# Three-branch decoder layer: idle transposes ahead of the first key products, key transposes tied behind twelve gate products, and a weight load that borrows the keys' buffer

## The chip, the core and the metric

The kernel runs on one core of one Trainium2 chip. The metric is the device time of one execution in microseconds; before the change it is 1395.42 us, the median of three runs.

## The reference, cut to what matters

One decoder layer over 1024 tokens of width 1024, in float32, with three token mixers side by side:

```python
h = rms_norm(x, g_norm)
proj = h @ w_in                       # split into the pieces named below
o_a = dsa_attention(q_a, k_a, v_a, q_i, k_i, w_i)   # 8 heads; a ReLU indexer picks the top 256 keys
o_b = causal_attention(q_b, k_b, v_b)               # 8 heads, low-rank q and kv, rotary part of 32
o_m = attention of q_m over 256 memory tokens       # 4 heads; k_m, v_m = rms_norm(mem) @ w_mem_kv
ys = [o_a * silu(z_a), o_b * silu(z_b), o_m * silu(z_m)]
branch[n] = ys[n] @ w_branch[n]
merged = sum over n of sigmoid(gate_logits[n]) * branch[n]
out = x + merged @ w_out
```

## The kernel before, in words

**Products.** Each float32 matrix is split into a high part and the rest (`wsplit`, line 242: ScalarE casts the high half, L243, VectorE or GpSimd subtracts for the low half, L246). A product is then three matmuls, high by high, high by low, low by high (`mm3`, L280 to L282). `wload` (line 248) takes a raw buffer from a pool, issues the loads on SyncE's queue (L260), takes two buffers for the halves and splits.

**Stages in order.** (1) The start: an identity matrix, 16 transposes of it into nowhere (L145), the memory tokens transposed (`norm_T`, L348, name `m`), the memory keys' products (`mkps`), the first four row blocks of x normalised and transposed (`x0tp`), the memory values' products (`mvps`), the rest of x, the memory queries. (2) The memory attention. (3) The latent projections of branch B and its queries. (4) Attention B (line 1047). (5) The indexer's projection and scores, and the first part of the top-k. (6) Branches M and B to the end, with the query/key/value projections of branch A (`qkv(p)`, line 1403, one for each of four pairs of heads) in between, and the top-k's steps spread over them on VectorE and ScalarE (`run_topk`). (7) Attention A (line 1596). (8) Branch A, and the output projection.

**Gate products.** The merge gates' logits have no order of their own and fill gaps of TensorE: `Filler.run(n)` (line 386) issues up to n products of 128 x 128 by 128 x 512, eight to a half job, and after eight ScalarE takes a tanh (L380) and SyncE stores it. A job is 16 products, and attention B has eight jobs, 128 products.

**`attention`** (line 545) serves B and A. Before its loop it generates the first pair's keys and values, calls `k_prep(0, 0)` (the first head's keys: eight transposes, L996 in B, L1525 in A, with copies) and `q_prep`, and runs gate products at four places in numbers given by a tuple, `PREB` or `PREA`:

```python
        for _ in load_ahead():
            fill.run(pre[0])
        ahead = load_ahead()
        fill.run(pre[1])
        k_prep(0, 0)
        fill.run(pre[2])
        q = q_prep(*units[0])
        fill.run(pre[3])
```

The loop has 33 steps; in B each runs three more gate products, and `fill.finish()` issues what is left. In B the keys of a pair come from the products `kv` (line 954); GpSimd multiplies them by their factors (L979, L981, tile `xk`).

**The last projection, `qkv(3)`.** Its weights come in four pieces (a3w0 to a3w3, three loads each) through two raw buffers, which the weights of the gate paths z use too, so a piece can be loaded only when the one two places before it has been split. Right behind it the keys of attention A's first pair are loaded (`load_k(0)`, line 1464, tile `akd`, tag `kd`, one buffer of 8 KB in each partition) and its queries (`load_q`, tile `aqs`), both tied behind the last of the weights' loads.

**What sets the order.** The program traces instructions in the order of the code; a scheduler then writes each engine's queue, by its own estimate of when an instruction is ready, so a gate product that stands later in the code can be issued before a transpose. `tc.issue_after(ins)` ties what a block issues on the engine of `ins` behind `ins`, in order only. Each engine works off its queue in order. A pool's tile with a tag of n buffers waits for the readers of the tile n places before it.

Of the kernel before, what the change touches and what calls it, by code (L numbers as in the profile page):

```python
# [11 lines left out]
F32 = mybir.dt.float32  # L12
# [11 lines left out]
P = 128  # L24
NT = S // P
# [9 lines left out]
WSM = [1]  # L35
WSB = [1]
WSI = [1]
PREB = (0, 0, 0, 16)
PREA = (0, 0, 4, 4)
NFQ = 2  # L40
PFQ = 4
NZG = 3
NWU = 16
WSF = [1]
WSO = [1]
ZB5 = 4
# [54 lines left out]
def hybrid_kernel(  # L101
# [5 lines left out]
    nc = tc.nc  # L107
    x, mem, out = x[0], mem[0], out[0]
    w_in, w_uq, w_ukv, w_mem_kv, w_branch, w_out = (
        w_in[0], w_uq[0], w_ukv[0], w_mem_kv[0], w_branch[0], w_out[0])  # L110
# [13 lines left out]
    def ps_t(nm, dt=F32):  # L124
        return pp.tile([P, 512], dt, tag="tp", name=nm, bufs=NTP)

    def ps_f(nm):
        return pp.tile([P, 512], F32, tag="fl", name=nm, bufs=1)
# [11 lines left out]
    ident = cp.tile([P, P], F32, name="ident")  # L140
    make_identity(nc, ident)
    identr = cp.tile([P, P], FR, name="identr")
    nc.vector.tensor_copy(identr, ident)
    for i in range(NWU):
        nc.tensor.transpose(ps_t(f"wu{i}")[:, 0:P], ident, ident)  # L145
    ones = cp.tile([P, 1], BF, name="ones")
    nc.vector.memset(ones, 1.0)
    mhalf = cp.tile([P, 128], F32, name="mhalf")
# [96 lines left out]
        eng = nc.vector if ws[wcount[0] % len(ws)] else nc.gpsimd  # L245
        eng.tensor_tensor(lo, raw, f(hi), op=ALU.subtract)  # L246

    def wload(pool, nm, srcs, a, n, kind=None):


        def tile(dt, tag, bufs, nm, width):
            if width is None:
                return pool.tile([P, a, n], dt, tag=tag, name=nm, bufs=bufs)
            t = pool.tile([P, width], dt, tag=tag, name=nm, bufs=bufs)
            return t[:, 0:a * n].rearrange("p (a n) -> p a n", a=a)
        width = pool_raw[2] if len(pool_raw) > 2 else None
        raw = tile(F32, "raw", pool_raw[0], nm + "r", width)
        o = 0
        for ap, w in srcs:
            last_load[0] = nc.sync.dma_start(raw[:, :, o:o + w], ap)  # L260
            o += w
        tag, bufs, width = kind or ("wp", pool_raw[1], width)
        hi = tile(FR, tag, bufs, nm + "h", width)
        lo = tile(FR, tag, bufs, nm + "l", width)
        if nm == "mkw0":
            for i in range(2):
                wsplit(hi[:, i], lo[:, i], raw[:, i])
        else:
            wsplit(hi, lo, raw)
        return hi, lo  # L270

    pool_raw = list(PRM)
# [3 lines left out]
    def wview(w, k0, a, c0, n):  # L276
        return w[k0 * P:(k0 + a) * P, c0:c0 + n].rearrange("(a p) c -> p a c", p=P)

    def mm3(ps, ah, al, bh, bl, start, stop):
        nc.tensor.matmul(ps, ah, bh, start=start, stop=False)  # L280
        nc.tensor.matmul(ps, ah, bl, start=False, stop=False)  # L281
        nc.tensor.matmul(ps, al, bh, start=False, stop=stop)  # L282

    def proj_w(nm, pool, w, cols, nk, per=None, held={}):

# [51 lines left out]
    def norm_T(xp, xs, tbs, gcol, dst, nm, scale=True):  # L337

        for tb, xt in zip(tbs, xs) if scale else ():
            r = sm.tile([P, 1], F32, tag="xr", name=f"{nm}r{tb}")  # L340
            row_factor(xp, xt, f"{nm}{tb}", r)
            eng = nc.gpsimd if tb in NXP else nc.vector
            eng.tensor_scalar(out=xt, in0=xt, scalar1=r, scalar2=None, op0=ALU.mult)
        n = len(tbs) * P
        for k in range(NK):
            tp = ps_t(f"{nm}tp{k}")
            for i, xt in enumerate(xs):
                nc.tensor.transpose(tp[:, i * P:(i + 1) * P], xt[:, k * P:(k + 1) * P], ident)  # L348
            hi, lo = dst(k)
            hi_ins.append(nc.scalar.activation(hi, tp[:, 0:n], AF.Copy, scale=gcol[:, k:k + 1]))  # L350
            nc.vector.scalar_tensor_tensor(out=lo, in0=tp[:, 0:n], scalar=gcol[:, k:k + 1], in1=f(hi),
                                           op0=ALU.mult, op1=ALU.subtract)
# [192 lines left out]
    def attention(gen, k_prep, q_prep, scores, pv, fill, per, pre, GEN, ldj):  # L545

        units = [(p, hh, G) for p in range(4) for hh in range(2) for G in GORD]
        pairs = iter(range(4))

        def load_ahead():  # L550
            p = next(pairs, None)
            if p is None:
                return iter(())
            g = gen(p)
            next(g)
            return g

        for _ in load_ahead():
            fill.run(pre[0])
        ahead = load_ahead()  # L560
        fill.run(pre[1])
        k_prep(0, 0)
        fill.run(pre[2])
        q = q_prep(*units[0])
        fill.run(pre[3])
        N = len(units)

        def fl(k):

            nonlocal ahead  # L570
            want = go + (GEN[j] - go) * sum(GF[:k + 1]) / sum(GF)
            while done[0] < want and next(g, 0) != 0:
                done[0] += 0.5
            if k == 4 and j == ldj:
                for _ in g:
                    pass
                ahead = load_ahead()
            fill.run(per[k])
        Sc, V = None, None
        for i in range(N + 1):  # L580
            j = i % 8
            if j == 0:
                g, done = ahead, [0]
            go = done[0]
            Sn = scores(*units[i], q) if i < N else None
            V = pv(*units[i - 1], Sc) if 1 <= i <= N else None
            if Sn:
                Sn.mm(0)
            if V:
                V.pt(0)  # L590
            fl(0)
            if Sn:
                Sn.exp(0)
                Sn.mm(1)
            if V and V.nk > 1:
                V.pt(1)
            fl(1)
            if Sn:
                Sn.exp(1)
                Sn.norm()  # L600
            if V:
                for kp in range(2, V.nk):
                    V.pt(kp)
                    fl(kp)
                    V.mmv(kp - 2)
                if V.nk > 1:
                    V.mmv(V.nk - 2)
            fl(4)
            if i < N:
                if j == KP1:  # L610
                    k_prep(units[i][0], 1)
                if j == 7 and i + 1 < N:
                    k_prep(units[i][0] + 1, 0)
                if i + 1 < N:
                    q = q_prep(*units[i + 1])
            fill.run(per[5])
            if V:
                V.mmv(V.nk - 1)
            if V:
                V.evac()  # L620
            Sc = Sn
        fill.finish()
# [8 lines left out]
    with ExitStack() as ph:  # L631
        wpool = ph.enter_context(tc.tile_pool(name="w1", bufs=3, reuse_waits="tile"))
# [30 lines left out]
        with ExitStack() as ph2:  # L663
# [52 lines left out]
            for i in range(2):  # L716
                raw = hT_first[i]
# [10 lines left out]
            for kp in range(NK // 2):  # L728
                raw = wpool.tile([P, 2, 544], F32, tag="raw", name=f"mvw{kp}", bufs=PRM[0])
# [16 lines left out]
            for h in range(4):  # L746
                tp = ps_t(f"kmt{h}")
# [6 lines left out]
        with ExitStack() as ph2:  # L754
# [19 lines left out]
            for j in range(2):  # L774
                for h in range(4):
                    tbs = range(4 * j, 4 * j + 4)
                    nm = f"m{h}_{j}"
                    tp = ps_t(nm + "q")
# [90 lines left out]
    with ExitStack() as ph:  # L869
        cb = ph.enter_context(tc.tile_pool(name="ckv", bufs=1, reuse_waits="tile"))  # L870
        ckv = [(cb.tile([P, S], FR, name=f"ckvh{i}"), cb.tile([P, S], FR, name=f"ckvl{i}")) for i in range(2)]
        with ExitStack() as ph2:
            wpool = wpool2
# [6 lines left out]
            wu = []  # L880
            for i in range(2):
                raw = wk.tile([P, 3, 384], F32, tag="uqr", name=f"uqr{i}", bufs=1)
# [10 lines left out]
            for tb in range(NT):  # L893
# [6 lines left out]
                for i in range(2):  # L900
                    ps = ps_turn(f"qb{tb}_{i}", QBB)[:, 0:384]
# [28 lines left out]
        wpool = ph.enter_context(tc.tile_pool(name="w2b", bufs=2, reuse_waits="tile"))  # L930
        pool_raw[:] = [1, 4]
        hd = ph.enter_context(tc.tile_pool(name="bheads", bufs=2, reuse_waits="tile"))
# [53 lines left out]
        def k_prep(p, hh):  # L986
            h = 2 * p + hh
            xk = st[p][0]
            xq = wk.tile([P, NT, 96], F32, tag="xq", name=f"xqp{h}")
            nc.sync.dma_start(xq, s_qb.rearrange("(t p) c -> p t c", p=P)[:, :, 96 * h:96 * h + 96])  # L990
            kTh = hd.tile([96, S], FR, tag="kTh", name=f"bkh{h}")
            kTl = hd.tile([96, S], FR, tag="kTl", name=f"bkl{h}")
            for j in range(2):
                tp = ps_t(f"bkt{h}_{j}")
                for i in range(4):
                    nc.tensor.transpose(tp[0:96, i * P:(i + 1) * P], xk[:, 4 * j + i, hh, :], ident)  # L996
                cs = slice(j * 512, (j + 1) * 512)
                nc.scalar.copy(kTh[:, cs], tp[0:96, :])
                nc.vector.tensor_tensor(kTl[:, cs], tp[0:96, :], f(kTh[:, cs]), op=ALU.subtract)
            st[p, hh] = (kTh, kTl, xq)  # L1000
# [193 lines left out]
    if True:  # L1194
        pool_raw[:] = [2, 8]

        with ExitStack() as ph2:
# [22 lines left out]
            for j in range(2):  # L1220
                v = xi[j][:, :, 0:576].rearrange("p t (h d) -> p t h d", h=9)
                rope(v[:, :, :, 0:16], cos_a[:, 4 * j:4 * j + 4, :], sin_a[:, 4 * j:4 * j + 4, :], 9, 8, ip, f"ir{j}")
                kd = wk.tile([P, 4, 2, 64], F32, tag="kd", name=f"kd{j}", bufs=1)
                nc.vector.tensor_copy(kd, xi[j][:, :, 512:576].unsqueeze(2).to_broadcast([P, 4, 2, 64]))
                tp = ps_t(f"kit{j}")
# [6 lines left out]
            for t in IORD:  # L1232
# [5 lines left out]
                n = (t + 1) * P  # L1238
# [129 lines left out]
    with w3s as ph:  # L1368
        wpool = wpool3
# [33 lines left out]
        def qkv(p):  # L1403
# [2 lines left out]
            c = P * p  # L1406
            cols = [(C_QA + c, P), (C_KA + c, P), (C_VA + c, P)]
            ws[:] = WSQ
            pieces = [wload(wpool, f"a{p}w{kp}", [(wview(w_in, 2 * kp, 2, c0, n), n) for c0, n in cols], 2, 384)
                      for kp in range(4)]  # L1410
            ws[:] = WSG
            last = last_load[0]
            for j in range(2):
# [276 lines left out]
```

## Time and profile before

| | us |
|---|---|
| runs | 1395.42, 1401.73, 1394.19 (median 1395.42) |
| profiled execution | 1400.19 |
| its span, first to last instruction | 1398.4 |
| TensorE busy in it | 1360.3 |
| VectorE, ScalarE, GpSimd busy | 956.2, 693.4, 212.6 |

Times of the trace count from the start of the span. The profiled execution is one of its own and slower than the median of the runs by 4.8 us, so sums worked out in it are carried over with care.

### The profile page before, as it was taken

What the parts mean: (1) busy time and instruction counts of PE and PEld (TensorE: products, weight loads), DVE (VectorE), ACT (ScalarE), POOL (GpSimd) and SP (SyncE); (2) the same over time, 40 slices, a digit from 0 to 9 for tenths busy, and PEclk for the clock granted to TensorE, in tenths of its full rate; (3) what the DMA queues carried; (4) which work ended last, traced back from release to release, by engine and by line L of the source; (5) the groups of instructions that cost most, each with busy time, mean ns of one, the idle gap of its engine ahead of it and who ended that gap; (6) DMA issues with size and microseconds to landing.
All of it is one profiled execution on the core that took longest, in us unless ns stands there. A gap on an engine that the chain in (4) does not pass through costs nothing.

```text
span 1398.4 us, 20877 instructions
## 1 busy us (share of the span) xinstructions
PE 1360.3 (97%) x7456; PEld 1170.3 (84%) x7456; DVE 956.2 (68%) x2349; ACT 693.4 (50%) x1522; POOL 212.6 (15%) x239
## 2 busy tenths in 40 slices
PE   8999999999999999999999999998999999999998
PEld 6998888878889888977898889788988888877787
DVE  5945445678888872288887777877868888858511
ACT  6635533256666653165665566433346666644200
POOL 2141003611101000000004102414220000004200
PEclk9999999999999999999999999999999999999999
DMA  8411222221111213011424741974352442157632
GB/s 272 117 46 53 78 62 69 105 79 43 57 43 43 64 42 120 5 49 39 129 75 167 240 111 49 222 170 128 114 181 69 121 131 66 52 188 237 210 105 68
DMA packets 155016, 147.46 MB, mean 105 GB/s; under 512 B 38048, under 2 KB 114848, under 8 KB 154912
## 3 DMA queue, kind: packets, MB, share of 16 engines
q1 hardware_dynamic: 146288, 123.57, 29.8%
q0 software_dynamic: 7008, 20.45, 4.9%
q10 hardware_dynamic: 1616, 2.10, 0.4%
q8 instruction: 59, 0.97, 0.3%
q14 instruction: 45, 0.37, 0.1%
HBM read 99.43 MB, written 46.66 MB: 104 GB/s over the span
## 4 chain that ended last, share of the span: by engine, by line
PE 65%; DVE 13%; DMA 7%; ACT 6%; issue 4%; POOL 3%; SPq 2%; DVEq 0%; ACTq 0%; POOLq 0%
PE f L280 6%; PE f L281 5%; PE f L282 5%; DVE kdj L1072 3%; PE o L282 2%; PE o L280 2%; PE o L281 2%; ACT kag L1078 2%; PE ixps L281 1%; PE ixps L282 1%; PE ixps L280 1%; DVE idx L1266 1%; PE b_3pt L477 1%; PE qmps L282 1%; PE qmps L281 1%
## 5 line engine op out<-in xcount | busy, mean ns | idle before, releaser
L1078 ACT ACTIVATE kag<-idx,kaT 128x896 bf16<-128x896 f32 (+2 forms) x96 | 83.0, 865 | 45.5 <-DVE kaT L1099 36.0
L1072 DVE TENSOR_SCALAR_CACHE_REDUCE kdj<-idx,kdT 128x1024 bf16<-128x1024 f32 (+2 forms) x96 | 92.5, 964 | 1.1
L280 PE MATMUL f<-hTh,f_0h 128*128 128x512 f32 x184 | 79.2, 431 | 1.6 <-ACT fo L380 0.9
L280 PE MATMUL f<-hTh,f_1h 128*128 128x512 f32 x184 | 76.0, 413 | 0.0
L281 PE MATMUL f<-hTl,f_1h 128*128 128x512 f32 x184 | 74.2, 403 | 0.0
L282 PE MATMUL f<-hTh,f_0l 128*128 128x512 f32 x184 | 74.0, 402 | 0.0
L282 PE MATMUL f<-hTh,f_1l 128*128 128x512 f32 x184 | 73.9, 402 | 0.0
L281 PE MATMUL f<-hTl,f_0h 128*128 128x512 f32 x184 | 73.6, 400 | 0.0
L1621 POOL TENSOR_TENSOR ac<-ac,tg 128x512 f32<-128x512 f32 x16 | 24.3, 1531 | 256.1 <-DMA wo_0r<-in_w_out_dram 238.4
L1660 DVE TENSOR_TENSOR xr<-o,xr 128x512 f32<-128x512 f32 x16 | 11.0, 690 | 60.6 <-PE o L282 60.6
L380 ACT ACTIVATE fo<-f 128x512 f32<-128x512 f32 x48 | 28.8, 600 | 37.9 <-PE f L282 34.1
L1260 ACT ACTIVATE irl<-is 128x512 f32<-128x512 f32 (+1 forms) x80 | 37.7, 527 | 15.4 <-DVE idx L1266 11.4
L280 PEld LDWEIGHTS f<-hTh,f_0h 128*128 128x128 f32 x184 | 35.2, 191 | 8.5 <-ACT fo L380 2.6
L1266 DVE SCALAR_TENSOR_TENSOR idx<-irl,wi,idx 128x1024 f32<-128x1024 f32 (+5 forms) x42 | 39.8, 949 | 1.9 <-ACT irl L1260 0.3
L282 PEld LDWEIGHTS f<-hTh,f_0l 128*128 128x128 f32 x184 | 35.0, 190 | 6.8
L282 PEld LDWEIGHTS f<-hTh,f_1l 128*128 128x128 f32 x184 | 34.7, 188 | 6.0
L281 PEld LDWEIGHTS f<-hTl,f_0h 128*128 128x128 f32 x184 | 35.3, 192 | 3.7
L281 PEld LDWEIGHTS f<-hTl,f_1h 128*128 128x128 f32 x184 | 34.7, 189 | 4.3
L280 PEld LDWEIGHTS f<-hTh,f_1h 128*128 128x128 f32 x184 | 34.7, 189 | 4.0
L1258 PE MATMUL is<-kih,iqT 128*128 128x512 f32 (+1 forms) x80 | 29.8, 377 | 2.3 <-ACT irl L1260 2.3
L1207 DVE TENSOR_SCALAR wi<-ixps 128x8 f32<-128x8 f32 x8 | 1.3, 166 | 42.6 <-ACT xi L1205 42.6
L1259 PE MATMUL is<-kil,iqT 128*128 128x512 f32 (+1 forms) x80 | 27.4, 354 | 0.0
(1247 smaller groups left out, 4770.8 us busy)
## 6 DMA issues: line engine op xcount, KB each, us to landing
s_tg<-fo SPq DMA_DIRECT2D x48, 256.0 KB, 2.0
tg<-s_tg SPq DMA_DIRECT2D x48, 256.0 KB, 4.4
f_0r<-in_w_in_dram SPq DMA_DIRECT2D x23, 256.0 KB, 2.9
f_1r<-in_w_in_dram SPq DMA_DIRECT2D x23, 256.0 KB, 3.2
xx<-in_x_dram SPq DMA_DIRECT2D x8, 512.0 KB, 8.7
osb<-s_o SPq DMA_DIRECT2D x16, 256.0 KB, 3.3
s_acc<-ab POOLq DMA_DIRECT2D x16, 256.0 KB, 5.0
s_acc<-am POOLq DMA_DIRECT2D x16, 256.0 KB, 6.5
```

Of the source, the lines that this page charges most:

```text
L280: nc.tensor.matmul(ps, ah, bh, start=start, stop=False)
L281: nc.tensor.matmul(ps, ah, bl, start=False, stop=False)
L282: nc.tensor.matmul(ps, al, bh, start=False, stop=stop)
L380: nc.scalar.activation(o, ps, AF.Tanh, scale=0.5)
L477: nc.tensor.transpose(tp[:, i, :], Pt[b][:, kt * P:(kt + 1) * P], ident)
L1072: nc.vector.tensor_scalar(out=junk, in0=idx[t], scalar1=T[:, i:i + 1], scalar2=0.0, op0=ALU.is_ge, op1=ALU.add, accum_out=cnt[:, i:i + 1])
L1078: nc.scalar.activation(junk, idx[t], AF.Sign, bias=T[:, i:i + 1], accum_out=cnt[:, i:i + 1])
L1258: nc.tensor.matmul(sp[:, 0:w], q_, kih[:, k0:k0 + w], start=True, stop=False)
L1259: nc.tensor.matmul(sp[:, 0:w], q_, kil[:, k0:k0 + w], start=False, stop=True)
L1260: nc.scalar.activation(rl[:, k0:k0 + m], sp[:, 0:m], AF.Relu)
L1266: i_ = nc.vector.scalar_tensor_tensor(out=acc[:, 0:n], in0=rl[:, 0:n], scalar=wc, in1=acc[:, 0:n], op0=ALU.mult, op1=ALU.add)
L1621: nc.gpsimd.tensor_tensor(ac, ac, tg, op=ALU.add)
```

## The change

Three edits. First, the 16 transposes at the start write one bank of PSUM (`idle`, of the kind used for gate products) instead of three in turn, and 14 more of them are issued inside the memory tokens' `norm_T`, on TensorE behind the transposes of its third column block (k = 2). Second, `PREB` goes from (0, 0, 0, 16) to (0, 12, 0, 7): twelve gate products stand ahead of `k_prep(0, 0)` in attention B, whose transposes are tied behind the last matmul of them, and seven behind `q_prep`. Attention A has 0 at that place and is not tied. Third, pieces 2 and 3 of the last projection's weights are loaded into a tile with the tag `kd`, the keys' buffer of attention A, instead of the two raw buffers.

```diff
-PREB = (0, 0, 0, 16)
+PREB = (0, 12, 0, 7)
+NWU2 = 14
...
-    for i in range(NWU):
-        nc.tensor.transpose(ps_t(f"wu{i}")[:, 0:P], ident, ident)
+    idle = ps_f("idle")
+
+    def idle_products(n):
+
+        for _ in range(n):
+            i_ = nc.tensor.transpose(idle[:, 0:P], ident, ident)
+        return i_
+
+    idle_products(NWU)
...
-    def wload(pool, nm, srcs, a, n, kind=None):
+    def wload(pool, nm, srcs, a, n, kind=None, raw=None):
...
-        raw = tile(F32, "raw", pool_raw[0], nm + "r", width)
+        if raw is None:
+            raw = tile(F32, "raw", pool_raw[0], nm + "r", width)
...
-        nc.tensor.matmul(ps, al, bh, start=False, stop=stop)
+        last_mm[0] = nc.tensor.matmul(ps, al, bh, start=False, stop=stop)
...
             for i, xt in enumerate(xs):
-                nc.tensor.transpose(tp[:, i * P:(i + 1) * P], xt[:, k * P:(k + 1) * P], ident)
+                i_ = nc.tensor.transpose(tp[:, i * P:(i + 1) * P], xt[:, k * P:(k + 1) * P], ident)
+            if k == 2 and nm == "m":
+                with tc.issue_after(i_.ins):
+                    idle_products(NWU2)
...
         fill.run(pre[1])
-        k_prep(0, 0)
+        with tc.issue_after(last_mm[0].ins) if pre[1] else ExitStack():
+            k_prep(0, 0)
...
-            pieces = [wload(wpool, f"a{p}w{kp}", [(wview(w_in, 2 * kp, 2, c0, n), n) for c0, n in cols], 2, 384)
-                      for kp in range(4)]
+            raws = [None] * 4
+            if p == 3:
+
+                t = hd.tile([P, NT, 2, 2, 64], F32, tag="kd", name="a3r", bufs=1).rearrange("p t h e d -> p (t h e d)")
+                raws[2:] = [t[:, i * 768:(i + 1) * 768].rearrange("p (a n) -> p a n", a=2) for i in range(2)]
+            pieces = [wload(wpool, f"a{p}w{kp}", [(wview(w_in, 2 * kp, 2, c0, n), n) for c0, n in cols], 2, 384,
+                            raw=raws[kp]) for kp in range(4)]
```

## Rows read from the trace of the kernel before

**Rows 1.** The page, part 1: busy us, share of the span, instructions.

```profile
PE 1360.3 (97%) x7456; PEld 1170.3 (84%) x7456; DVE 956.2 (68%) x2349; ACT 693.4 (50%) x1522; POOL 212.6 (15%) x239
```

**Rows 2.** Waits of TensorE, longest first: total us, times, longest us.

```profile
PE a L281 <- DVE a3w3l L246: 5.5, 1, 5.5
PE mkps L280 <- ACT mTh L350: 3.2, 1, 3.2
PE bkt L996 <- POOL xk L981: 2.5, 1, 2.5
```

**Rows 3.** Stretches: length, busy PE, PEld, DVE, ACT, POOL; PEclk, DMA, GB/s.

```profile
980.00:985.00 5.00, 4.14 (x13) 4.14 (x14) 4.96 (x9) 0.84 (x2) 1.01 (x2) 0.52 1.05 346
...
285.00:290.00 5.00, 3.02 (x10) 2.54 (x11) 2.72 (x8) 1.10 (x3) 3.76 (x4) 0.73 0.18 52
```

**Rows 4.** Timeline of TensorE around 980 us: start, us, instruction, [idle before].

```profile
975.05 0.34 PE L280 MATMUL a<-a3w3h,hTh 128*128 128x384 f32 x1
980.86 0.69 PE L281 MATMUL a<-a3w3l,hTh 128*128 128x384 f32 x1 [5.46 <-DVE a3w3l L246]
...
987.09 0.34 PE L282 MATMUL a<-a3w2h,hTl 128*128 128x384 f32 x1
...
988.85 0.34 PE L280 MATMUL a<-a3w0h,hTh 128*128 128x384 f32 x1
```

**Rows 5.** Timeline of SyncE's queue, 930 to 975 us.

```profile
934.61 1.65 SPq L260 DMA_DIRECT2D a3w1r<-in_w_in_dram  x3
...
966.64 1.39 SPq L260 DMA_DIRECT2D a3w3r<-in_w_in_dram  x3
968.14 5.07 SPq L1469 DMA_DIRECT2D akd<-s_ka  x4
```

**Rows 6.** Timeline of TensorE: branch B's last product, attention A's first key transposes.

```profile
912.59 0.40 PE L282 MATMUL br<-yh,b1w7l 128*128 128x512 f32 x1
...
1026.02 1.03 PE L1525 MATMUL akt<-ident,akd 128*128 128x128 f32 x8
```

**Rows 7.** Timeline of TensorE at attention B's first key transposes.

```profile
282.95 0.39 PE L280 MATMUL f<-hTh,f_0h 128*128 128x512 f32 x1
...
284.24 0.28 PE L282 MATMUL kv<-ukv0h,ckvl 128*128 128x256 f32 x1
286.98 0.81 PE L996 MATMUL bkt<-ident,xk 128*96 128x128 f32 x4 [2.46 <-POOL xk L981]
287.44 0.78 PE L280 MATMUL f<-hTh,f_0h 128*128 128x512 f32 x1
...
291.12 0.39 PE L280 MATMUL f<-hTh,f_1h 128*128 128x512 f32 x1
...
292.28 0.39 PE L282 MATMUL f<-hTh,f_1l 128*128 128x512 f32 x1
```

**Rows 8.** Timeline of GpSimd: the rope part of those keys.

```profile
285.79 1.14 POOL L981 TENSOR_TENSOR xk<-kro,kf 128x256 f32<-128x256 f32 x1
```

**Rows 9.** Timeline of ScalarE at the end of attention B.

```profile
528.10 0.60 ACT L380 ACTIVATE fo<-f 128x512 f32<-128x512 f32 x1 [3.17 <-PE f L282]
528.59 1.16 ACT L243 CAST ixw0h<-ixw0r 128x1168 fp32r<-128x1168 f32 x1
```

**Rows 10.** Timeline of TensorE (PEld: weight loads) at the start.

```profile
1.47 3.27 PEld L145 LDWEIGHTS wu<-ident 128*128 128x128 f32 x16 [1.47 <-POOL ident masks.py:199]
...
9.64 0.80 PE L280 MATMUL mkps<-mkw0h,mTh 128*128 128x512 f32 x1 [3.18 <-ACT mTh L350]
...
13.65 0.63 PE L282 MATMUL mkps<-mkw0h,mTl 128*128 128x512 f32 x1
14.07 0.48 PE L280 MATMUL mkps<-mkw1h,mTh 128*128 128x512 f32 x1
```

**Rows 11.** The chain that ended last, 15 to 30 us: start, us, what.

```profile
19.94 6.82 DMA mvw<-in_w_mem_kv_dram
...
27.45 0.86 PE mvps L280 x2
```

More of the change, by code (lines that the diff above doesn't have):

```diff
@@ L281, in mm3 @@
         nc.tensor.matmul(ps, ah, bl, start=False, stop=False)
-        nc.tensor.matmul(ps, al, bh, start=False, stop=stop)
+        last_mm[0] = nc.tensor.matmul(ps, al, bh, start=False, stop=stop)
+    last_mm = [None]
     def proj_w(nm, pool, w, cols, nk, per=None, held={}):
```

## The prediction

> **What bounds the kernel now.** I read the engines' busy shares first, then TensorE's waits, then the granted clock by stretch, and only then the order of single instructions. TensorE is busy for 1360.3 of 1398.4 us [rows 1], so a stage gets shorter only where TensorE waits or runs at its lower clock. Its three longest waits are 5.5, 3.2 and 2.5 us [rows 2], and each part of the change lies ahead of one of them: the late weights of the last query/key/value projection, the memory keys' first products, and the first key transposes of attention B. After two of these waits the granted clock is low: 0.52 in 980 to 985 us and 0.73 in 285 to 290 us [rows 3], which are stretches with a part at the lower of the two levels, 1.2 GHz. So each wait has a second price behind it.
>
> The profiled execution took 1400.19 us (span 1398.4, 1.8 around it). The median of the three runs, 1395.42 us, is 4.8 below it. I make the sum on the profile and carry it over to the median at the end.
>
> **Part 1, the late weight pieces.** One of the projection's products begins at 975.05; the next would follow 0.176 us later (ten begin between 987.09 and 988.85), but begins at 980.86 [rows 4]. That is 5.6 us lost. From there 19 matmuls take 6.23 us (980.86 to 987.09) instead of 19 x 0.176 = 3.3: another 2.9 us at the lower clock. What it waited for is the low half of piece 3, which stood behind other work in VectorE's queue [rows 2, 4]. The piece was late from the start: piece 1 was issued from 934.61 to 936.3, piece 3 only at 966.64 [rows 5], because the two raw buffers had to be split first. With raw buffers of their own in the keys' tile, pieces 2 and 3 (six DMAs, the same bytes, none added) can be loaded right behind piece 1: that tile's space last held tiles read at 912.59 [rows 6]. Their data is then there some 30 us before the use at 975, and their splits can run right behind those of pieces 0 and 1. I take the whole 8.5 us; its bounds are 0, if VectorE's queue still holds the split back, and 8.5.
>
> What is late next: the first keys' load. It now waits until both pieces have been split out of its buffer, and what stands behind it in SyncE's queue waits too. It was issued at 968.14 [rows 5], and its first reader is at 1026.02 [rows 6], 1017.5 once TensorE is 8.5 us ahead; a split near 968 leaves it there. So I cost it at nothing: the cover is some 45 us of projection.
>
> **Part 2, twelve gate products ahead of the key transposes.** The last value product begins at 284.24 and takes its 0.12 us of pitch; the transposes begin at 286.98 [rows 7], a delay of 2.6. They wait for GpSimd, which ends the keys' rope part at 286.93 [rows 8]. Before the change sixteen gate products (three matmuls each) follow the transposes in the program, and the scheduler had already moved nine of them ahead: a half job of eight, and a ninth at 282.95 [rows 7]. Now twelve must go ahead: three more, nine matmuls at 0.232 us (291.12 to 292.28, five of them, [rows 7]), 2.1 us of work in the gap, with 0.5 us of wait left. The gap also cost clock: nine matmuls take 3.68 us from 287.44 to 291.12 [rows 7] instead of 2.1, so 1.6 us. The seven products left behind the transposes are as many as were left there before, so the second half of the keys and the first scores keep their cover. In all 19 products are taken ahead of the loop instead of 16; 99 go with the 33 steps, so 10 instead of 13 remain of 128 for the end. There the first cast of the indexer's weights, at 528.59, stands right behind a gate's tanh that waited for TensorE [rows 9], and moves up with it; the 2.1 us taken out there is thus gained and not turned into a wait. The part is worth 2.1 + 1.6 = 3.7; bounds 0 (the end waits for weights instead) and 3.7.
>
> **Part 3, the idle transposes.** Sixteen are moved to another bank and cost what they did. Fourteen more stand behind the sixth memory transpose; at the start's pitch (3.27 us for sixteen loads, 0.204 each) they take 2.9 us, inside the wait of 3.18 us before the first key product at 9.64 [rows 10]. So they cost nothing while that wait lasts, and up to 2.9 if the data were there at once, which this profile excludes. Their possible gain: the products from 9.64 to 14.07 come at the lower level's pitch (0.42 us from 13.65 to 14.07 [rows 10], against 0.23 [rows 7]); at the full clock these 4.4 us would be 2.2 shorter. I take 0 for the end time, and keep 2.2 as the bound, because the stage after it doesn't wait for TensorE: the value products begin at 27.45 behind a cast and a load that was issued at 19.94 and landed 6.82 us later [rows 11]. TensorE would reach that wait earlier and wait longer.
>
> A row bears on whether the clock rises at all: sixteen transposes in a row from 1.47 us were followed by products still at the lower pitch [rows 10]. The Trainium skill, "TensorE: Matmul & The Clock Gate", section "Part 4: PE-mode transpose", says that transposes do not bring on the full clock as matmuls do; by that rule this term is 0 for a second reason, and the rival below that makes it 2.2 falls away. The row agrees as far as it reaches; no run here shows a longer row of transposes.
>
> **The sum.** 8.5 + 3.7 + 0 = 12.2 us on the profile. Of this 7.7 us (5.6 + 2.1) is waiting, which I expect in every run; 4.5 us (2.9 + 1.6) is clock. The three runs span 7.5 us and the profiled one lies 4.8 above their median, so I take it (an estimate) that the median run loses only half of that clock: 7.7 + 2.2 = 9.9, and 1395.42 - 9.9 = **1385.5 us**.
>
> **The rivals.**
> *The top-k takes over* (0.16). VectorE is busy 4.96 of 5 us from 980 [rows 3] with the rest of the top-k, and ScalarE's copies of TensorE's results stand in one queue with its passes. TensorE 8.5 us early could meet them. Against it: the projection writes to five banks, four tiles of some 4.2 us (24 x 0.176) of slack. If 4 to 7 us of part 1 came back as waits, the gain is 3 to 6: 1389.5 to 1392.5.
> *The late split stays late* (0.08): the change doesn't do what it says, because the scheduler writes VectorE's queue by its own estimates, as it did when the split came after 975. Then part 2 alone remains, 2.1 + 0.8: 1392.5.
> *The keys' load becomes the late one* (0.08), the case on the other side. Place: SyncE's queue behind the third piece's split. Its four issues took 5.07 us [rows 5]; if they go behind a load that waits for TensorE's next stage, the first key transposes wait, and each us after 1017.5 costs one. To end over 0.5% slower (7 us) it must also eat the 9.9: the keys would have to land after 1034. It would end at 1402.5 or more, a us for each us. Against it speak the 58 us between issue and use now.
> *The start pays too* (0.08): the idle transposes lift the clock and the shorter key products bring the first row normalisation forward, up to 2.2 us: 1383.3, and 1381 with all the clock of the other parts. I give it little, since two things must go right: the clock must rise, and the wait at 27.45 must give way.
>
> **How the numbers follow.** The forecast has 0.60. By about 0.5% (7 us, what a measurement of this kernel can tell from no change), faster means under 1388.4. The forecast reaches from 1383.2 (all 12.2) to 1389 (hardly any clock, 1 us of part 2 lost): 0.56 of its 0.60 are faster. With the start's 0.08: 0.64. Same: 0.04 + 0.16 + 0.08 = 0.28. Slower: 0.08. The range 1380 to 1392 holds the forecast, the start's case and nearly all of the top-k's, some 0.82.
>
> **What would show it.** Part 1: pieces 2 and 3 loaded before 945, their low halves before 972, no wait of TensorE near 975, and a granted clock of 1.00 from 970 to 1000. It is wrong if a wait of several us stands at the projection under another name, or before the first key transposes of attention A. Part 2: 36 gate matmuls before the first of those transposes, a wait there under 1 us, a clock of 1.00, and the indexer's first product earlier than before by some 3 us, with nothing new waiting there. Part 3: 14 transposes between 6.5 and 9.5 us, and the value products still at about 27.5 us; if those move, I sized it wrong. The forecast as a whole is wrong if the first scores of attention A come less than 7 us earlier.

## The result and the profile after

The changed kernel takes 1408.82 us (median of 5 runs, 1404.87 to 1410.33) against 1397.26 us of the kernel before on the same chip (5 runs, 1394.19 to 1404.06). The ratio, taken over all these runs, is 1.0063, 95% interval 1.0042 to 1.0083: slower by about 0.6% (the medians alone are 11.6 us, 0.8%, apart), where 0.7% faster was forecast and the range ended at 1392. The profiled execution after took 1404.87 us (span 1403.1), the shortest of its five runs; that of before took 1400.19 (span 1398.4), 2.9 above the median of its runs. So the two traces differ by 4.7 us only, and what follows places these 4.7 and not the whole difference of the medians.

TensorE's longest waits in the changed kernel (the view of rows 2; the columns are total us, times, longest us), longest first:

```profile
PE br L289 <- DVE am L1414: 4.3, 1, 4.3
PE f L289 <- DVE sz L1318: 3.5, 1, 3.5
PE a L290 <- DVE a3w0l L254: 2.9, 1, 2.9
...
PE f L289 <- ACT fo L394: 2.4, 5, 0.6
...
PE bkt L1011 <- DVE xk L996: 1.1, 1, 1.1
...
PE bkt L1011 <- POOL xk L996: 0.4, 1, 0.4
```

The waits that headed [rows 2] are gone (0.4 us is left of the third), and three others head the list: for am (VectorE's product of a gate with a result of branch B's output, which empties the bank), for sz and for a3w0l. The projection now waits for piece **0** (a3w0l), which was not late before, and attention A's first gate product (f) waits for the gate path's evacuation (sz). The granted clock shows the same by stretch (columns as in rows 3):

```profile
285.00:290.00 5.00, 3.98 (x19) 2.67 (x17) 2.60 (x9) 2.16 (x5) 4.05 (x5) 1.00 0.18 52
975.00:980.00 5.00, 2.13 (x7) 1.96 (x7) 4.96 (x6) 3.42 (x8) 0.00 (x0) 0.62 0.25 70
980.00:985.00 5.00, 5.00 (x23) 5.00 (x22) 5.00 (x14) 2.27 (x4) 2.24 (x2) 0.70 0.83 206
1030.00:1035.00 5.00, 3.72 (x14) 3.24 (x15) 3.08 (x7) 2.16 (x4) 3.53 (x6) 0.66 0.30 110
```

The stretch from 285 has its full clock now (0.73 in [rows 3]), the projection still has not, and attention A's start has lost it.

**A ledger of the two traces.** I took the starts of the same instructions from the two timelines of TensorE; the lag is after minus before.

| first or last instruction | before | after | lag |
|---|---|---|---|
| last memory-key product | 23.75 | 22.92 | -0.83 |
| first score of attention B | 294.56 | 292.57 | -1.99 |
| end of the indexer's projection | 586.80 | 585.33 | -1.47 |
| first product of branch B's output | 866.59 | 866.14 | -0.45 |
| last product of that output | 912.59 | 916.66 | +4.07 |
| first product of the last projection | 971.89 | 974.74 | +2.85 |
| its last product | 1014.01 | 1015.81 | +1.80 |
| first score of attention A | 1032.00 | 1039.44 | +7.44 |
| last product of the kernel | 1394.08 | 1398.75 | +4.67 |

The projection takes 41.07 us instead of 42.12: part 1 brought 1.05 of its 8.5. It waits 5.3 us in all (0.7 for a3w0h, 2.9 for a3w0l, 1.7 for ScalarE's copies) where it waited 5.5 before. Right behind it 5.64 us are lost. The +4.5 at branch B's output is the wait for am (4.3 us against 1.2) and the clock behind it; the section on e1 and e2 comes back to it. Behind attention A the traces differ by what that stretch varies by: from A's last score to the end it takes 163.1 us before, 160.4 after, and 160.4 to 167.3 over the twelve traces of this study.

**Where the lag begins.** SyncE's queue of the changed kernel around the last projection's loads (start us, us to issue, instruction):

```profile
927.77 2.80 SPq L269 DMA_DIRECT2D a3r<-in_w_in_dram  x5
930.69 0.61 SPq L1495 DMA_DIRECT2D aqs<-s_qa  x1
...
937.68 1.40 SPq L269 DMA_DIRECT2D a3w1r<-in_w_in_dram  x3
939.12 0.53 SPq L1495 DMA_DIRECT2D aqs<-s_qa  x1
939.75 0.64 SPq L418 DMA_DIRECT2D f_0r<-in_w_in_dram  x1
945.34 0.37 SPq L418 DMA_DIRECT2D f_1r<-in_w_in_dram  x1
949.53 0.37 SPq L418 DMA_DIRECT2D f_0r<-in_w_in_dram  x1
...
980.62 3.27 SPq L1489 DMA_DIRECT2D akd<-s_ka  x4
```

Pieces 2 and 3 (a3r) are issued from 927.77 on, as forecast (piece 3 was at 966.64 in [rows 5]). But with them came something that the forecast did not have: the first **gate weights of attention A** (f_0r, f_1r). In the kernel before they were issued like this:

```profile
981.33 0.80 SPq L404 DMA_DIRECT2D f_0r<-in_w_in_dram  x1
```

The reason is two lines of the attention A phase that the diff does not touch (1594 and 1595 of the kernel before): `with tc.issue_after(a3.ins): fill_a.run(1)`. Like the keys and the queries, the first gate weights are tied behind the last load of the projection's weights. That load moved up, and they moved with it. They go through one raw buffer of their own, so each load waits until the one before it has been split. ScalarE's queue in the changed kernel:

```profile
943.96 0.62 ACT L251 CAST f_0h<-f_0r 128x512 fp32r<-128x512 f32 x1 [6.54 <-DMA f_0r<-in_w_in_dram]
944.49 0.26 ACT L1451 COPY a_0xq<-a 128x128 f32<-128x128 f32 x1
...
948.16 0.62 ACT L251 CAST f_1h<-f_1r 128x512 fp32r<-128x512 f32 x1 [3.07 <-DMA f_1r<-in_w_in_dram]
...
952.52 0.62 ACT L251 CAST f_0h<-f_0r 128x512 fp32r<-128x512 f32 x1 [3.24 <-DMA f_0r<-in_w_in_dram]
...
953.51 0.74 ACT L1120 ACTIVATE kas<-idx,kaT 128x512 bf16<-128x512 f32 x1
...
971.41 0.62 ACT L1475 CAST a_0qs<-a_0xq 128x512 fp32r<-128x512 f32 x1 [7.67 <-POOL a_0xq L1473]
...
973.81 0.88 ACT L251 CAST a3w0h<-a3w0r 128x768 fp32r<-128x768 f32 x1
```

Three casts (f_0h, f_1h, f_0h) stand ahead of the projection's copies and the top-k's pass (kas), and ScalarE stands still 6.5, 3.1 and 3.2 us for their DMAs. In the kernel before this pass stood at 940.30:

```profile
940.30 0.74 ACT L1105 ACTIVATE kas<-idx,kaT 128x512 bf16<-128x512 f32 x1
```

It is thus 13.2 us later, while TensorE was 2.9 later. The Trainium skill, "PSUM — Partial Sum Buffer", section "Engine vs sequencer instructions", says that the queues of ScalarE, VectorE and GpSimd are worked off strictly first in, first out; the trace agrees, for the last product that a_0xq's copy needs began at 932.97 and the copy still began at 944.49, behind the cast. From there everything in the two queues is 12.9 us late: the normalisation (the cast a_0qs), the casts of all four pieces behind it, and with them the splits on VectorE:

```profile
977.06 0.93 DVE L254 TENSOR_TENSOR a3w0l<-a3w0r,a3w0h 128x768 fp32r<-128x768 f32 x1
...
979.65 0.95 DVE L254 TENSOR_TENSOR a3w3l<-a3r,a3w3h 128x768 fp32r<-128x768 f32 x1
```

In the kernel before a3w0l was split at 964.12, some 8 us ahead of the projection's first product (971.89), and only a3w3l was late [rows 4]:

```profile
964.12 0.93 DVE L246 TENSOR_TENSOR a3w0l<-a3w0r,a3w0h 128x768 fp32r<-128x768 f32 x1
```

Now the four splits run from 977.06 to 980.6, behind the projection's first product, which now begins at 974.74. TensorE meets the first of them, and later the gate path's evacuation:

```profile
978.05 0.69 PE L290 MATMUL a<-a3w0l,hTh 128*128 128x384 f32 x1 [2.87 <-DVE a3w0l L254]
...
1031.28 0.80 PE L289 MATMUL f<-hTh,f_0h 128*128 128x512 f32 x1 [3.48 <-DVE sz L1318]
...
1032.72 1.78 PE L1545 MATMUL akt<-ident,akd 128*128 128x128 f32 x8
```

The eight transposes akt take 1.78 us at the lower clock (1.03 in the kernel before). The wait of 3.5 us and the lower clock behind it (0.66 in 1030 to 1035) make up most of the 5.6 us of the ledger.

### The profile page after: what moved, and what is told of

It is laid out like the page before. It is cut to its first block, busy times and chain, and to the rows that moved or that the text cites. A ratio compares the mean times of both kernels' runs of the same rounds, so it can differ in the third digit from the quotient of the medians.

```text
span 1403.1 us, 20890 instructions
## 1 busy us (share of the span) xinstructions
PE 1361.3 (97%) x7470; PEld 1170.5 (83%) x7470; DVE 957.2 (68%) x2349; ACT 692.8 (49%) x1522; POOL 211.0 (15%) x239
## 4 chain that ended last, share of the span: by engine, by line
PE 61%; DVE 14%; ACT 7%; DMA 6%; issue 5%; POOL 4%; SPq 1%; DVEq 0%; ACTq 0%; POOLq 0%
PE f L289 6%; PE f L291 5%; PE f L290 5%; DVE kdj L1087 3%; PE o L291 2%; PE o L290 2%; PE o L289 2%; ACT kag L1093 2%; PE ixps L291 1%; DVE idx L1281 1%; PE ixps L289 1%; PE ixps L290 1%; PE qmps L291 1%; PE qmps L290 1%; PE qmps L289 1%
```

## The experiments

Theory G: the loss comes from the gate weights of attention A, which moved up by their tie to the moved load. Rivals: parts 2 and 3 cost it (P), the keys' buffer costs it (K). In each table row the ratio is to the kernel before on the same chip, and the kernels of one group ran on one chip.

| run | us | ratio, 95% interval |
|---|---|---|
| before (first group) | 1400.55 | |
| e1 without part 1 | 1401.76 | 1.0006 (0.9990 to 1.0021) |
| e2 part 1 only | 1410.42 | 1.0066 (1.0046 to 1.0087) |
| e3 gate weights tied late | 1400.10 | 1.0000 (0.9984 to 1.0016) |
| e4 gate weights tied early, alone | 1411.58 | 1.0081 (1.0055 to 1.0106) |
| before (second group) | 1401.34 | |
| e5 e3 and the bank freed | 1396.63 | 0.9966 (0.9948 to 0.9985) |
| e6 the bank freed, alone | 1402.36 | 0.9998 (0.9980 to 1.0016) |
| e7 e5 without parts 2 and 3 | 1395.03 | 0.9954 (0.9936 to 0.9972) |
| e8 e5 with 12 and 4 gate products | 1397.08 | 0.9970 (0.9957 to 0.9984) |
| before (third group) | 1401.93 | |
| e9 loads early, casts late, bank freed | 1397.43 | 0.9964 (0.9950 to 0.9977) |
| e10 the change and the bank freed | 1407.53 | 1.0035 (1.0019 to 1.0050) |

### Which part costs it: e1 and e2

e1 is the changed kernel with the last projection's pieces as before; e2 is the kernel before with part 1 alone:

```diff
-            pieces = [wload(..., raw=raws[kp]) for kp in range(4)]
+            pieces = [wload(...) for kp in range(4)]
```

> The changed kernel without part 1: the last projection's pieces 2 and 3 go through the two raw buffers again; parts 2 and 3 stay. Theory G (the loss comes from part 1: the first gate weights of attention A are tied behind the last weight load of the projection, which now comes some 35 us earlier, and their three casts stand in ScalarE's queue ahead of the copies and the top-k): the loss is gone, time within 2 us of before, 1 us or so less than before from attention B; ScalarE's first gate cast is back behind 980 us, and the wait of 5 to 6 us for a3w3l near 975 us is back. Rival P (parts 2 and 3 cost it: the wait at 897 us for branch B's output that is new in the changed kernel): 4 us or more slower than before, with that wait of 4 us at 897 in the trace.

> The kernel before with part 1 alone. Theory G: as slow as the changed kernel, 7 to 12 us over before; three gate casts between 939 and 953 us on ScalarE, the top-k's pass over 896 columns at about 970 us instead of 959.5, TensorE waiting 2 to 5 us for a3w0l near 975 and again 2 to 4 us before attention A. Rival P (parts 2 and 3 cost it): 0 to 8 us faster than before.

As G had it: without part 1 the loss is gone, with part 1 alone it is all there. So P is out as the cause of the loss. e1 has the wait for am too (3.5 us) at the time of before, so that wait is not what makes the changed kernel slower. Nor is it new: e4, which has no part of the change, has 3.8 us of it. Over the twelve traces it is 1.2 us twice (before and e6, which have no part of the change either) and 2.3 to 4.3 ten times; whether a part of the change makes it more frequent, one trace of each kernel can't tell. It is behind ScalarE's cast of one weight piece of branch B (b1w6), whose load took 8.8 us from its issue to the cast before and 11.5 after. The clock stays at 1.00 behind the two waits of 1.2 us and falls behind the ten others (0.50 to 0.61 in 902 to 905 us in nine of them; in e5 0.78 there and 0.65 in 905 to 908). Why that load varies was not tried.

The traces place part of the loss of part 1. From the projection's first product to attention A's first score e2 takes 64.9 us and the changed kernel 64.7; the three traces that load the pieces as before and tie nothing early take 60.1 (before), 58.0 (e6) and 57.4 (e1). So 4.8 to 7.6 us of the 9 to 10 by which e2 is slower lie there; where the rest lies no trace shows.

### The tie or the buffer: e3, e4 and e9

e3 moves only the tie: the gate weights go behind the load of the last gate path.

```diff
         early(2, NZG)
+        zl = last_load[0]
...
-        with tc.issue_after(a3.ins):
+        with tc.issue_after(zl.ins):
             fill_a.run(1)
```

> The changed kernel with one line moved: the first gate weights of attention A are tied behind the last gate-path weight load (z, w = 2), not behind the projection's last weight load. The weights still go through the keys' buffer. Theory G: the casts of the gate weights come behind those of the pieces again, no wait of TensorE over 1 us between 960 and 1020 us, granted clock 1.00 from 970 to 1000, and the time is 6 to 9 us under before, about 1389 us (what the prediction had for part 1, 8.5, less what stays of other waits). Rival K (the keys' buffer itself costs it: the keys' load has to wait for the splits, and the queue behind it): no gain, 5 us or more over before, with the wait at the first key transposes of attention A. Rival P: 4 us of the gain missing because of the wait at 897.

Half right: the gain of 6 to 9 us did not come. The projection did what the prediction said: 974.04 to 1007.57 from its first product to its last, 33.53 us against 42.12, so 8.6 us won where 8.5 had been worked out; no wait, and the clock of 980 to 985 is 1.00 (0.52 in [rows 3]):

```profile
980.00:985.00 5.00, 5.00 (x30) 5.00 (x30) 4.80 (x11) 2.43 (x6) 1.55 (x4) 1.00 0.49 189
```

The keys' load, my candidate for what is late next, was issued at 970.56, 2.4 us later than in [rows 5] and 53 before its use: K is out. Yet the time was that of before: 5.8 of the 8.6 were given back between the projection's end and attention A's first score, and the 2.8 left don't show in the median, whose interval leaves 2 us either way. GpSimd, VectorE and TensorE of e3 there:

```profile
1018.38 2.93 POOL L244 TENSOR_TENSOR a_1rr<-a_1rr,mhalf 128x16 f32<-128x16 f32 x1
...
1021.35 0.69 DVE L1473 TENSOR_TENSOR a_1xk<-a_1xk,a_1rr 128x512 f32<-128x512 f32 x1 [1.59 <-POOL a_1rr L244]
...
1022.23 0.68 DVE L1318 SCALAR_TENSOR_TENSOR sz<-sz,z 128x512 f32<-128x512 f32 x1
...
1022.96 0.50 PE L289 MATMUL f<-hTh,f_0h 128*128 128x512 f32 x1 [3.48 <-DVE sz L1318]
```

The evacuation sz at 1022.23 stands on VectorE behind the last rows' normalisation, and that waits for GpSimd's power (2.93 us). In the kernel before it was at 1022.62:

```profile
1022.62 0.69 DVE L1303 SCALAR_TENSOR_TENSOR sz<-sz,z 128x512 f32<-128x512 f32 x1
```

TensorE is 6.4 us earlier, this chain is not: it hangs on the top-k and the normalisations in the two queues, not on TensorE. Before, the gate product came at 1025.33, behind it; now it waits.

e4 does the reverse, in the kernel before: its pieces and buffers stay, only the gate weights' tie goes to the load of piece 1.

```diff
+                if kp == 1:
+                    half[0] = last_load[0]
...
-        with tc.issue_after(a3.ins):
+        with tc.issue_after(half[0].ins):
             fill_a.run(1)
```

> The kernel before with nothing changed but that tie: the first gate weights of attention A are tied behind the load of piece 1 of the last projection's weights instead of piece 3; pieces 2 and 3 go through the two raw buffers as before, the keys' buffer isn't touched. Theory G: slower than before by 8 to 18 us, more than the changed kernel, since the splits that free the raw buffers are 13 us late and pieces 2 and 3 are loaded only behind them: the top-k's pass over 896 columns at about 970 us, waits of TensorE for a3w0l and then for a3w2l or a3w3l, 10 us together. Rival K (the keys' buffer costs it): within 2 us of before.

The tie alone makes the kernel before 11 us slower. Its waits near the projection are those that G named:

```profile
PE a L281 <- DVE a3w3l L246: 5.8, 1, 5.8
PE a L281 <- DVE a3w0l L246: 2.9, 1, 2.9
PE a L281 <- DVE a3w2l L246: 2.6, 1, 2.6
PE a L280 <- ACT a3w2h L243: 1.9, 1, 1.9
```

e9 tells the loads from the casts: the tie stays early, and a second one holds the casts (with the banks of e5, below).

```diff
+        c3 = split_hi[n_hi + 3]
...
-        with tc.issue_after(a3.ins):
+        with tc.issue_after(a3.ins), tc.issue_after(c3.ins):
```

> The changed kernel with the banks of e5 and with the gate weights of attention A still tied behind the projection's last weight load, but also, on ScalarE, behind the cast of its piece 3. The first gate load is thus issued early, near 940 us, but no gate cast stands ahead of the copies and the top-k; ScalarE's queue is that of e5. Theory G (it is the place of the casts in ScalarE's queue that costs, not the early loads): the time of e5, 1395 to 1398, 4 us or so under before. Rival L (the early load itself, or SyncE's queue behind it, costs it): 5 us or more over before.

The load is issued at 939.83 as in the changed kernel, its cast comes behind the pieces', the top-k's pass over 896 columns is at 962.61 (972.40 in the changed kernel), and the time is that of e5:

```profile
939.83 0.63 SPq L418 DMA_DIRECT2D f_0r<-in_w_in_dram  x1
```
```profile
962.61 1.06 ACT L1120 ACTIVATE kas<-idx,kaT 128x896 bf16<-128x896 f32 x1
...
972.38 0.60 ACT L251 CAST f_0h<-f_0r 128x512 fp32r<-128x512 f32 x1
```

So it is the place of the casts in ScalarE's queue, and of the splits behind them in VectorE's, which move with them. Only the first load is early here; the second waits for the one raw buffer until 986.25, so what three early loads would cost without early casts was not tried.

### What gives the gain back: e5, e6, e10

The gate products of attention A write one bank of PSUM, and an accumulator of the last gate path had used it. e5 is e3 with other banks for that path; e6 the same in the kernel before; e10 in the changed kernel. The order of no queue changes.

```diff
-            pz.append(ps_turn(f"z{n}_{w}_{j}", ZB))
+            pz.append(ps_turn(f"z{n}_{w}_{j}", ZB if (n, w) != (0, 2) else [ps_mm, ps_s]))
```

> The kernel of e3 (gate weights tied late), and the two accumulators of the last gate path (z, w = 2) take other banks than the one that the gate products of attention A use. No queue's order changes. Theory N (in e3 the 8 us won at the projection are given back at attention A's first gate product: it waits 3.5 us for VectorE to empty its bank, behind the last rows' normalisation, whose chain through ScalarE, VectorE and GpSimd ends at 1022 us in the kernel before and in e3 alike, and some 1.9 us more go at the lower clock): that wait is gone, the first key transposes follow the gate path at once, 1394 to 1396 against 1400.5 of before, 4 to 6 us faster than e3. Rival Q (attention A can't start earlier anyhow, since its keys, masks or stores are late too): another wait of 3 us or more within 10 us, and the time of e3, 1400.

> The kernel before with the banks of e5 alone. Theory N: no change (within 1.5 us), since there the gate product comes 2.7 us after its bank is empty (1022.6 against 1025.3). Rival B (the bank costs a wait in the kernel before too): 3 us or more faster.

> The changed kernel with the banks of e5 alone; the gate weights stay tied early. Theory G, split in two: the wait for a3w0l near 975 us with its lower clock stays, the wait of 3.5 us at attention A's first gate product with its lower clock goes. So it should be 4 to 6 us faster than the changed kernel and still 3 to 6 us slower than before. Rival: as slow as the changed kernel, 8 to 10 us over before, with another wait before the first scores of attention A.

All three came out near what N and G gave: e5 4.7 us under before (1396.6, where 1394 to 1396 was expected), e6 no change, e10 5.6 us over before, where 3 to 6 was expected. In e5 the transposes follow at once and at the full clock:

```profile
1023.29 1.03 PE L1546 MATMUL akt<-ident,akd 128*128 128x128 f32 x8
```

From the projection's end to attention A's first score the stretch takes 20.1 us (1010.88 to 1030.96), 18.0 in the kernel before and 23.6 in the changed one. Of the 2.1 us still missing 1.5 are a wait for VectorE's copy of the queries, behind the same chain. e10 splits the loss: the changed kernel's ratio of 1.0063 falls to 1.0035. That is some 4 us (0.28% of 1402), though the two intervals overlap and come from different groups of runs; in the traces the stretch falls from 23.6 to 18.9 us. In e10 the projection takes 42.3 us, as before, with the wait for a3w0l (2.9) in it. Against e3 and e5, whose projection takes 33.5, that is 8.8 us of gain not had. Of the 4.9 us that e10 loses against before (0.35%), its trace places 1.1 to 3.9: 61.2 us from the projection's first product to attention A's first score against the 57.4 to 60.1 above.

### What parts 2 and 3 are worth: e7 and e8

e7 is e5 without them; e8 is e5 with the gate products of attention B counted otherwise:

```diff
-PREB = (0, 12, 0, 7)
+PREB = (0, 12, 0, 4)
```

> The kernel before with part 1, the gate weights tied late and the banks of e5, without parts 2 and 3. Theory S (parts 2 and 3 are worth nothing at the end): as e5, within 1.5 us, 1394 to 1396.5. Rival (they gain the 3.7 us of the prediction): 3 to 4 us slower than e5.

> e5 with 12 and 4 gate products around the key transposes of attention B instead of 12 and 7, so that 16 products as before are taken ahead of the loop and ScalarE's tanh falls at the same steps of the loop as in the kernel before. Theory W (part 2's gain is lost again in attention B because three more products shift the half jobs against the steps: TensorE waits five times 0.5 us for the tanh that empties the one gate bank): those waits are gone in attention B and the time is 1 to 2 us under e5. Rival C (the seven products behind the transposes are needed as cover for the first scores): a wait of 0.7 us or more before attention B's first scores, and no gain over e5.

e7 is the fastest kernel of the study, 6.3 us under before; its interval and that of e5 overlap, so parts 2 and 3 bring nothing that can be told. e8 says where part 2's gain goes. The three waits for the tanh inside attention B are gone, as W had it: from attention B's first score to the indexer's first product it takes 239.0 us, against 240.8 to 241.0 in the six traces with 12 and 7 and 238.7 to 238.9 in the five without part 2. The time is not the 1 to 2 us under e5 that W had: the two medians are 0.5 us apart, e8 the slower. At the indexer's projection e8 waits for a weight piece:

```profile
540.76 0.64 PE L289 MATMUL ixps<-ixw3h,hTh 128*128 128x320 f32 x1 [2.72 <-ACT ixw3h L251]
```

The load of that piece was issued at 531.82 and its cast began at 539.54, when it had landed. This is one trace; that this load would be late in each run, and eat the gain there, was not tried.

## Why the prediction was wrong

**The step that failed** is in part 1, "What is late next: the first keys' load. ... So I cost it at nothing." The question was right and the list was short. I asked what waits for the moved buffer and what stands behind it in SyncE's queue; I did not ask what else is *tied* to the load that I moved. Three blocks were tied to it: keys, queries and the first gate weights. Each of the last brings a cast into ScalarE's queue and a split into VectorE's, and those were moved 42 to 46 us up (the first load from 981.33 to 939.75), ahead of the copies and the top-k. The price was 9.2 us for part 1 alone (e2, 0.66% of 1400.55) where a gain of 8.5 was forecast.

**Part 1's sum** was right as far as it went: e3 shows 8.6 us at the projection, waiting and clock together. But it was the sum of one trace: in e1 and e6, which load the pieces as before, the wait for a3w3l is 4.2 and 4.6 us instead of 5.5 and the projection takes 39.3 and 40.1 us, so the same move is worth 5.8 to 8.6. The bounds of 0 to 8.5 were wrong: nothing in the trace of before excluded a loss, and I had looked for one in a single queue.

**The rival "top-k takes over"** was the second thing to happen, and it had 0.16. I held against it that the projection writes to five banks. The bank that decided was the gate products' one, two stages later, and what held it was the normalisation behind the top-k: of the 8.6 us won in e3, 5.8 went there. The rival on the slower side was the right kind (a tie to the moved load) at the wrong place (the keys).

**Part 2** did locally what was said, less one thing. Nine more matmuls went ahead, the first transposes waited 0.4 us (0.5 forecast), the clock of 285 to 290 is 1.00, but the second half of the keys then waited 1.1 us for VectorE. At attention B's first scores 2.1 of the 3.7 us were there (lag -1.99 from +0.14). At the indexer's first product none was left (533.47 against 533.42): 1.5 us went in three waits for the tanh (0.5 each), since 19 products ahead of the loop instead of 16 put the emptying of the one gate bank at other steps; the rest is not placed. The lag of -1.47 at the end of that projection is mostly waits for its weights, which the trace of before had (0.6 and 0.5) and that of after not. The forecast had looked for the loss only behind the loop. That the indexer's weights could be the next wait was its bound of 0; e8 shows that wait.

**Part 3** cost nothing and brought nothing, as said: at 96.6 us the lag is +0.15. That the last key product is 0.83 us earlier and the first value product 0.9 (26.54) is not its doing: e2, which does not have it, shows the same (22.86 and 26.54), and over the traces without part 3 the last key product is at 22.8 to 23.8, with it at 22.9 to 24.1. Why it brings nothing was argued only in part rightly: the clock did rise, but the key products also began later (last section).

**The forecast's test** was that the first scores of attention A come 7 us earlier or it is wrong. They came 7.4 later. Both signs that part 1 was wrong came too: a wait at the projection under another name (a3w0l), and one ahead of attention A's first key transposes (sz).

## What to carry to other kernels

When a load is moved, list what is tied to it or ordered behind it, not only what it waits for; then follow each of these into every queue it feeds, casts and splits too. A cast that waits for its DMA at the head of an in-order queue delays all the work behind it, however little it costs itself: here three of 0.6 us held two engines back by 13. And a stage that is made 8 us shorter gains only down to the next chain that does not depend on it; look for the bank or buffer where the two meet, and free it with the same change.

## What the runs showed of the hardware that was not expected

**Idle transposes do lift TensorE's clock.** The prediction weighed a rule of the Trainium skill, "TensorE: Matmul & The Clock Gate", section "Part 4: PE-mode transpose", by which transposes do not bring on the full clock as matmuls do. The start of the changed kernel:

```profile
1.47 3.67 PE L150 MATMUL idle<-ident 128*128 128x128 f32 x16 [1.47 <-POOL ident masks.py:199]
4.94 1.64 PE L359 MATMUL mtp<-ident,mx 128*128 128x128 f32 x6
6.37 1.92 PE L150 MATMUL idle<-ident 128*128 128x128 f32 x14
9.93 1.22 PE L359 MATMUL mtp<-ident,mx 128*128 128x128 f32 x6 [1.63 <-DVE mTl L365]
10.90 0.49 PE L289 MATMUL mkps<-mkw0h,mTh 128*128 128x512 f32 x1
11.23 0.40 PE L290 MATMUL mkps<-mkw0l,mTh 128*128 128x512 f32 x1
```

The first sixteen take 0.23 us each, the fourteen 0.14, before any product has run: that is near the ratio of the akt transposes at the two levels (1.78 and 1.03 for eight). The key products that follow begin at the full pitch (0.23 us) after a wait of 1.63. This is read from the pitch, since the granted clock reads 1.00 for the first 7 us of every trace, also where the pitch is low. In two traces with sixteen idle and six real transposes, and no product before, the granted clock itself shows the fall, so the upper level had been there. In e2 the first products have the short pitch after a wait of 2.46 us, and then the clock goes from 0.96 (9.1 to 10.1) to 0.50. In e4 it goes from 1.00 (6 to 7) to 0.50 (8 to 9), inside the wait of 3.5 us, and the products begin at the low pitch. The low pitch of the first products before [rows 10] is thus, as far as these two show, not for want of a rise; it came behind the wait of 3.18 us. For these float32 transposes the measurement decides against the rule.

```profile
9.13 0.50 PE L281 MATMUL mkps<-mkw0h,mTh 128*128 128x512 f32 x1 [2.46 <-ACT mTh L351]
9.47 0.39 PE L282 MATMUL mkps<-mkw0l,mTh 128*128 128x512 f32 x1
...
10.44 0.78 PE L283 MATMUL mkps<-mkw0h,mTl 128*128 128x512 f32 x1
```
```profile
9.10:10.10 1.00, 0.96 (x3) 0.49 (x4) 1.00 (x3) 0.71 (x2) 0.00 (x0) 0.96 1.05 404
10.10:11.00 0.90, 0.90 (x3) 0.73 (x4) 0.73 (x2) 0.75 (x1) 0.00 (x0) 0.50 1.06 394
```

The raised clock did not always last until the key products. In four of the seven traces with the fourteen transposes (after, e3, e5, e10) the products begin at the full pitch, behind waits of 1.5 to 2.3 us; in e1, e8 and e9, behind waits of 2.0 to 3.1, the granted clock falls to 0.50 there. Nor was anything won where it lasted: in the changed kernel the key products begin 1.3 us later than before, since the remaining memory transposes now wait for VectorE ahead of them, and they end when kernels without part 3 end them too.
